# Hybrid decoder block on one core: the mixer's weight sums made beside the state space, one weight piece in its own place, norms in two steps

## The chip, the cores and the metric

One core of a Trainium2 chip runs the whole kernel. The metric is the device time of one execution in microseconds. The kernel before was timed in three runs; beside them stands one profiled execution, from which all lines of the profile are taken. The core has five instruction queues that run by themselves: TensorE (PE, matrix products into PSUM banks), VectorE (DVE), ScalarE (ACT), GpSimd (POOL) and SyncE (SP, which here only issues transfers). Transfers are issued on SP's and on ACT's queue and run on the core's 16 DMA engines. Each queue holds its instructions in a fixed order, and an instruction that waits holds back all behind it.

## The reference

One decoder layer on 1024 tokens of width 1024, in float32. The part around the change:

```python
u = rms_norm(h, norm_mix[l])
u_ssm, q, k, v, f_logit, gate_logits = jnp.split(u @ w_in[l], [...], axis=-1)
y_ssm = jax.nn.gelu(s5_ssm(u_ssm, ...))                  # diagonal state space, 32 groups
glu_a, glu_b = jnp.split(y_ssm @ w_glu[l], 2, axis=-1)
out_a = glu_a * jax.nn.sigmoid(glu_b)
out_b = forgetting_attention(q, k, v, f_logit + b_forget[l]) @ w_fox_o[l]
gate_a, gate_b = jnp.split(jax.nn.sigmoid(gate_logits), 2, axis=-1)
h = h + (gate_a * out_a + gate_b * out_b) @ w_mix_out[l]  # the mixer projection
h = h + memory_cross_attention(rms_norm(h, norm_mem_q[l]), ...)
f_a, f_b = jnp.split(rms_norm(h, norm_ffn[l]) @ w_ffn_in[l], 2, axis=-1)
h = h + (jax.nn.silu(f_a) * f_b) @ w_ffn_out[l]           # then a last rms_norm
```

## The kernel before

Tokens are kept in 8 tiles of 128 rows, or turned, features on the 128 partitions and tokens in two halves of 512. Every float32 product is made of three products of rounded parts: each operand is split into a high part (ACT rounds it, L178) and a low part (DVE subtracts, L179), and PE does high times high, low times high, high times low (L168 to L170; L602 in the mixer). A weight comes by `wload`: SP fetches it into a tile `raw` (two of them), ACT and DVE split it into `whi` and `wlo`. These two have a few slots each, so a split waits until PE has read the weight that had the slot.

Four stages follow each other. `stage_in` makes the norm and the first projections. `stage_ssm` makes the 32 gate blocks, 16 columns of 128 in two halves, each 24 matmuls of 512 columns, and hangs the state space (S5, four quarters q) between them: the table `todo` names the block ahead of which a step of S5 is written. In a quarter the transposes (`turn_weights`) give `Ts`, which three transfers on SP shift into a Toeplitz matrix, ACT copies it to `Tt` (L1427); `states` fetches `xg` and lets PE multiply it (L1440), DVE makes the recurrence; `out` multiplies `Tt` and `xg`. Fox (the forgetting attention) is next, and `stage_tail` does the rest.

`stage_tail` begins with a loop over j = 0 to 7 that makes the gated units (`glu`; `value` empties PE's bank with the DVE copy at L1166, `sigmoid` multiplies, L1172) and, three steps behind, the Fox projection `fox_part`, which adds the gated halves to `sg` and splits the result into the operands of the mixer. The mixer projection is a 2 x 2 block product with seven products instead of eight (`mix_mm(n, i)`: product n, block i of 4; `mix_add` adds it to the residual tiles H). Four of the products need sums of quarters of `w_mix_out`. They are made in the loop's first steps: `mix_fetch` reads two 512 KB pieces into the tiles with the tags `gbc` and `xs`, `mix_sums` adds quarters on DVE (L544) and ACT's queue stores them to `sums_d`, from where `mix_weights` loads them later like any weight. Both tiles have one slot, so the fetch of a step waits for the stores of the step before, and later uses of these tiles (`xm`, `s4`, the row `xs` of a norm) follow.

The last Fox parts, 5, 6 and 7, are woven into product 1. In parts j > 3 the second half's add runs on POOL (L564). The products then come in the order 1, 2, 6, 5, 3, 7, 4, and after each block one piece of `side` is written: the preparation of two columns of the forward network's weights (`ahead`: fetch `wpr`, sums on POOL, splits `wph` and `wpl` in slots of the pool `tmp`, stores to `w_d` on ACT's queue). The RMS norms ahead of the memory attention (`norm`) scale a row of H into `xs` on DVE (L217) and turn it on PE (L223). The norms of tiles 0 to 3 are written behind every second block of products 7 and 4, those of tiles 4 to 7 among the query projections.

## Time and profile before

| | us |
|---|---|
| median of 3 runs | 1615.45 (1613.74 to 1618.33) |
| the profiled execution | 1621.55 |
| its span, first to last instruction | 1619.8 |
| PE busy | 1534.7 (95%) |
| DVE busy | 1064.4 (66%) |
| ACT busy | 670.2 (41%) |
| POOL busy | 268.8 (17%) |
| mean granted clock of TensorE | 0.975 |

A row of the timeline has start, length, engine, line, operation, output <- inputs, shapes, and in brackets the idle time ahead of it on its engine and what ended it. A row of the waits has who waited and for whom, the total, how often, and the longest. A row of the windows has the stretch, its length, busy time and instructions of PE, PE's weight loads, DVE, ACT and POOL, then TensorE's granted clock, the busy share of the DMA engines and GB/s. The chain of waits has start, length and what it was. On SP a row spans the issues that it groups, with the waits between them.

### The profile page before, as it was taken

The page shows a single profiled execution, that of the slowest core. Times are in us where ns is not written, and L with a number is a line of the kernel's source. Part 1 is how long each engine was busy: PE and PEld are TensorE (multiplying, and loading weights), DVE is VectorE, ACT ScalarE, POOL GpSimd, SP SyncE. Part 2 cuts the span into 40 slices and gives each one's busy share as a digit, 9 for nine tenths or more (in the row PEclk, how much of TensorE's full clock was granted, in tenths as well). Part 3 has the DMA queues.
Part 4 walks back from the last instruction along what each step waited for, and adds up shares of the span by engine and source line. Part 5 has one row for each costly group of instructions (what it writes and reads, how often), then busy time and mean ns, then how long its engine had stood idle before and what let it go on. Part 6 is the DMA issues. An engine that isn't in the chain of part 4 may idle for free.

```text
span 1619.8 us, 20543 instructions
## 1 busy us (share of the span) xinstructions
PE 1534.7 (95%) x7301; PEld 1263.2 (78%) x7301; DVE 1064.4 (66%) x1882; ACT 670.2 (41%) x1191; POOL 268.8 (17%) x341
## 2 busy tenths in 40 slices
PE   5799999999999999697999999999999999999997
PEld 5688888898776678586787777888888888788886
DVE  5756555444777777687765687766766776466555
ACT  5422433323666642123445564333333333254342
POOL 3015443200211124123201210000100000000001
PEclk8899999999999999898999999999999999999999
DMA  8745446442124646857813168444454444796642
GB/s 268 141 93 92 126 131 113 120 137 29 34 43 72 170 127 205 289 186 282 275 53 104 53 223 303 149 150 156 157 166 159 150 162 149 241 393 231 195 156 104
DMA packets 202871, 258.71 MB, mean 160 GB/s; under 512 B 36024, under 2 KB 127064, under 8 KB 202256
## 3 DMA queue, kind: packets, MB, share of 16 engines
q1 hardware_dynamic: 193840, 237.47, 49.4%
q10 hardware_dynamic: 8928, 19.93, 3.2%
q8 instruction: 57, 0.93, 0.2%
q14 instruction: 46, 0.38, 0.1%
HBM read 176.08 MB, written 83.20 MB: 160 GB/s over the span
## 4 chain that ended last, share of the span: by engine, by line
PE 76%; DMA 7%; DVE 7%; issue 4%; ACT 3%; POOL 2%; SPq 1%; ACTq 0%; DVEq 0%; POOLq 0%
PE mm L947 15%; PE pv L947 7%; PE mm L168 7%; PE mm L169 7%; PE mm L170 7%; PE mm L1084 4%; PE sc L947 4%; PE sc L1084 3%; PE pv L1084 3%; PE sc L168 3%; PE sc L169 3%; PE sc L170 3%; PE misc L1084 1%; DMA mw<-in_w_mix_out_dram 1%; DMA or<-in_w_ffn_out_dram 1%
## 5 line engine op out<-in xcount | busy, mean ns | idle before, releaser
L179 DVE TENSOR_TENSOR wlo<-raw,whi 128x1024 fp32r<-128x1024 f32 (+2 forms) x127 | 138.3, 1093 | 115.4 <-ACT whi L178 114.8
L178 ACT CAST whi<-raw 128x1024 fp32r<-128x1024 f32 (+1 forms) x128 | 116.6, 914 | 169.9 <-PE mm L169 49.2
L168 PE MATMUL mm<-uh,whi 128*128 128x512 f32 x344 | 138.2, 402 | 2.4 <-ACT whi L178 2.3
L170 PE MATMUL mm<-uh,wlo 128*128 128x512 f32 x344 | 135.7, 395 | 0.0
L179 DVE TENSOR_TENSOR ol<-or,oh 128x1024 fp32r<-128x1024 f32 x73 | 89.4, 1224 | 70.5 <-ACT oh L178 69.4
L169 PE MATMUL mm<-ul,whi 128*128 128x512 f32 x344 | 135.7, 394 | 0.0
L178 ACT CAST oh<-or 128x1024 fp32r<-128x1024 f32 x73 | 76.7, 1051 | 104.4 <-PE mm L1084 35.0
L979 POOL TENSOR_TENSOR g<-a,c 128x512 f32<-128x512 f32 x22 | 35.6, 1617 | 397.2 <-ACT a L978 397.2
L1709 POOL TENSOR_TENSOR pl<-pf,ph 128x512 fp32r<-128x512 f32 (+1 forms) x32 | 39.5, 1234 | 243.1 <-DVE ph L1708 198.1
L168 PEld LDWEIGHTS mm<-uh,whi 128*128 128x128 f32 x344 | 65.5, 191 | 14.8 <-ACT whi L178 2.8
L170 PEld LDWEIGHTS mm<-uh,wlo 128*128 128x128 f32 x344 | 65.2, 190 | 14.6 <-DVE wlo L179 1.3
L169 PEld LDWEIGHTS mm<-ul,whi 128*128 128x128 f32 x344 | 65.5, 190 | 10.9
L197 POOL TENSOR_TENSOR r<-ms,mhalf 128x1 f32<-128x1 f32 (+1 forms) x30 | 17.8, 598 | 317.5 <-DVE ms L193 287.4
L1706 ACT ACTIVATE pf<-sc 128x512 f32<-128x512 f32 (+1 forms) x96 | 46.4, 490 | 49.6 <-DVE sc L1702 30.0
L947 PE MATMUL pv<-S3h,we 128*128 128x512 f32 x176 | 58.1, 389 | 0.0
L168 PE MATMUL mm<-yh,whi 128*128 128x512 f32 x104 | 41.7, 401 | 14.1 <-DVE sg L1166 14.1
L1179 POOL TENSOR_TENSOR sg<-sg,ga 128x512 f32<-128x512 f32 x16 | 30.3, 1919 | 87.0 <-DMA ga<-gate_d 43.8
L1712 DVE TENSOR_TENSOR pl<-pf,ph 128x512 fp32r<-128x512 f32 (+2 forms) x64 | 35.7, 558 | 10.1 <-ACT ph L1711 9.4
L170 PE MATMUL mm<-yh,wlo 128*128 128x512 f32 x104 | 41.3, 398 | 0.0
L169 PE MATMUL mm<-yl,whi 128*128 128x512 f32 x104 | 41.3, 397 | 0.0
L1084 PE MATMUL mm<-oh 128*128 128x512 f32 x106 | 41.3, 389 | 0.0
L1084 PE MATMUL mm<-ol,oh 128*128 128x512 f32 x106 | 41.3, 389 | 0.0
(667 smaller groups left out, 4615.4 us busy)
## 6 DMA issues: line engine op xcount, KB each, us to landing
or<-c_d SPq DMA_DIRECT2D x77, 256.0 KB
wo<-in_w_ffn_out_dram SPq DMA_DIRECT2D x22, 512.0 KB
c_d<-g SPq DMA_DIRECT2D x44, 256.0 KB
t_d<-wo SPq DMA_DIRECT2D x44, 256.0 KB
or<-t_d SPq DMA_DIRECT2D x44, 256.0 KB
raw<-in_w_ffn_in_dram SPq DMA_DIRECT2D x20, 512.0 KB
rawb<-in_w_ffn_in_dram SPq DMA_DIRECT2D x20, 512.0 KB
raw<-in_w_in_dram SPq DMA_DIRECT2D x18, 512.0 KB
```

What stands on the lines that cost most here:

```text
L168: T.matmul(ps, lh, rh, start=first, stop=False)
L169: T.matmul(ps, lh, rl, start=False, stop=False)
L170: T.matmul(ps, ll, rh, start=False, stop=last)
L178: self.A.copy(hi, src)
L179: (self.G if pool_lo else self.V).tensor_sub(lo, src, f32(hi))
L947: T.matmul(ps, l_[:, k, :], r_, start=first and k == 0 and i == 0, stop=k == 3 and i == 2, skip_group_check=True)
L979: G.tensor_mul(g[:, 512:], a1, c1)
L1084: T.matmul(ps, l_[:, gi], r_[:, 512:], start=n < 3 and p == 0 and k == 0 or n == 7 and p == 0 and k == 0, stop=p == NP - 1 and k == 2, ski ...
L1179: self.B.G.tensor_mul(self.out[j][:, cs], self.out[j][:, cs], ga)
L1706: self.exp = A.activation(pf[:, off:], ps[:, off:], AF.Exp)
L1709: G.tensor_sub(pl[:, off:], pf[:, off:], f32(ph[:, off:]))
L1712: V.tensor_sub(pl[:, off:], pf[:, off:], f32(ph[:, off:]))
```

## The change

The mixer's weight sums move from the first four steps of the loop in `stage_tail` to `stage_ssm`: ahead of gate block 7k stands the fetch of piece pair k, ahead of 7k + 2 its adds, ahead of 7k + 3 its stores, now on SP's queue. They have two tiles of their own there. To make room for them, tables that only the setup of S5 uses move to the pool that ends with `stage_in`. In the mixer, the first weight piece of product 1 gets tiles of its own (`w1h`, `w1l`), the loads of product 2's weight are written ahead of Fox part 7, the POOL add of the Fox parts becomes a DVE add, and the split of S1 is held back to the next part. A norm is cut in two: `scaled` (the DVE part, now into a slot of `tmp`) right behind the last sum of its tile, `turned` (the PE part) in product 7 and among the query projections. PE's count of matmuls is the same.

```diff
-    def wload(self, pieces, cols, pool_lo=False, behind=None):
+    def wload(self, pieces, cols, pool_lo=False, behind=None, into=None):
 
         raw = self.wpool.tile([P, RAW], F32, tag="raw", bufs=2, name="raw")
         for off, shape, src in pieces:
             n = shape[0] * shape[1]
             self.S.dma_start(raw[:, off:off + n].rearrange("p (k c) -> p k c", k=shape[0]), src)
-        hi = self.wpool.tile([P, WSLOT], F32R, tag="whi", name="whi")
-        lo = self.wpool.tile([P, WSLOT], F32R, tag="wlo", name="wlo")
+        hi, lo = into or [self.wpool.tile([P, WSLOT], F32R, tag=t_, name=t_) for t_ in ("whi", "wlo")]
...
+    mw = {}
+
+    def mix_fetch(k):
+        mw[k] = [qp.tile([P, D], F32, tag="mw", bufs=2, name="mw") for _ in range(2)]
+        for w_, r_ in zip(mw[k], (k, 4 + k)):
+            S.dma_start(w_, w_mix_out[r_ * P:(r_ + 1) * P, :])
+
+    def mix_parts(k):
+        (b11, b12), (b21, b22) = [(w_[:, :512], w_[:, 512:]) for w_ in mw[k]]
+        return (5, b11, b12), (7, b12, b22), (6, b22, b11), (4, b21, b22)
+
+    def mix_sums(k):
+
+        for _, o, i in mix_parts(k):
+            B.V.tensor_add(o, o, i)
+
+    def mix_store(k):
+        for n, o, _ in mix_parts(k):
+            S.dma_start(sums_d[n, k // 2][:, k % 2 * 512:k % 2 * 512 + 512], o)
+
...
+    for k in range(4):
+        for i, f in ((7 * k, mix_fetch), (7 * k + 2, mix_sums), (7 * k + 3, mix_store)):
+            todo.setdefault(i, []).append(lambda f=f, k=k: f(k))
     for i, f in enumerate(gates):
         for g in todo.get(i, []):
             g()
...
-    def mix_fetch(k):
-        mw[k] = [s2.tile([P, D], F32, tag=t_, bufs=1, name="mw") for t_ in ("gbc", "xs")]
-        for w_, r_ in zip(mw[k], (k, 4 + k)):
-            S.dma_start(w_, w_mix_out[r_ * P:(r_ + 1) * P, :])
-
-    def mix_sums(k):
-
-        w1, w2 = mw.pop(k)
-        b11, b12, b21, b22 = w1[:, :512], w1[:, 512:], w2[:, :512], w2[:, 512:]
-        for n, o, i in ((5, b11, b12), (7, b12, b22), (6, b22, b11), (4, b21, b22)):
-            V.tensor_add(o, o, i)
-            A.dma_start(sums_d[n, k // 2][:, k % 2 * 512:k % 2 * 512 + 512], o)
...
-            (G if j > 3 and h else V).tensor_add(sg[:, cs], sg[:, cs], gb)
+            if h and late:
+                late.pop(0)()
+            V.tensor_add(sg[:, cs], sg[:, cs], gb)
...
-        give("S1", bslot, k, x_[:, 512:])
         S.dma_start(s3_d[k // 2][:, k % 2 * 512:k % 2 * 512 + 512], s0)
+        late.append(lambda: give("S1", bslot, k, x_[:, 512:]))
...
-                hl = B.wload([(0, (2, 512), src)], D)
+                own = [s2.tile([P, D], F32R, tag=t_, bufs=1, name=t_) for t_ in ("w1h", "w1l")] if n == 1 and kk == 0 else None
+                hl = B.wload([(0, (2, 512), src)], D, into=own)
...
-    mix_fetch(0)
     for j in range(8):
         if j > 3:
             for f in glu.values(j):
                 f()
         glu.rest(j)
-        if j < 4:
-            mix_sums(j)
-            if j < 3:
-                mix_fetch(j + 1)
...
     fox_part(6)
     mix_mm(1, 2)
+    mix_weights(2)
     fox_part(7)
-    mix_weights(2)
...
-    def norm(t, gb, act, banks=("misc", "pv")):
-        xs = s2.tile([P, D], F32, tag="xs", bufs=1, name="xs")
-        B.norm_scale(xs, H[t], B.rstd(H[t]), gb)
-        B.norm_turn(xs, act, t, banks)
+    xss = {}
+
+    def scaled(t):
+        xss[t] = tmp("xs")
+        B.norm_scale(xss[t], H[t], B.rstd(H[t]), gq)
+
+    def turned(t, banks):
+        B.norm_turn(xss.pop(t), u2, t, banks)
...
     for n, m in ((2, 5), (6, 3), (5, 7), (3, 4), (7, None), (4, None)):
         for i in range(4):
             mix_mm(n, i)
-            if n in (7, 4):
-                if i % 2:
-                    norm(2 * (n == 4) + i // 2, gq, u2, ("mm", "misc"))
+            if n == 7:
+                turned(i, ("mm", "misc"))
+            mix_add(n, i)
+            if n in (3, 4):
+                scaled((n == 4) * 4 + i)
+            elif late:
+                late.pop()()
             elif side:
                 side.pop(0)()
-            mix_add(n, i)
...
-    weave([lambda h=h: mem_q(h, 0) for h in range(MH)], [lambda t=t: norm(t, gq, u2) for t in range(4, 8)])
+    weave([lambda h=h: mem_q(h, 0) for h in range(MH)], [lambda t=t: turned(t, ("misc", "pv")) for t in range(4, 8)])
...
-            self.rows = sp.tile([48, P], F32, name="prow")
+            self.rows = self.xp.tile([48, P], F32, name="prow")
...
```

Where instructions stand now is shown at three places, in the order of one engine's queue. The first is SP's queue in `stage_ssm`, in the first two quarters: `raw` are the gates' weights, `mw` the pieces of `w_mix_out`, `y_d` the quarter's output. Before:

```order
L153 DMA raw_1378<-in_w_in_dram 128x4x256
L1433 DMA xg_1412<-u_d_77 128x1024
L153 DMA raw_1646<-in_w_in_dram 128x4x256
L153 DMA raw_1652<-in_w_in_dram 128x4x256
L1422 DMA Ts_1366<-Ts_1366 112x128
L1422 DMA Ts_1366<-Ts_1366 96x256
L1422 DMA Ts_1366<-Ts_1366 64x512
L153 DMA raw_1976<-in_w_in_dram 128x4x256
L153 DMA raw_1982<-in_w_in_dram 128x4x256
L1433 DMA xg_1828<-u_d_77 128x1024
```

With the change, from the first shift of `Ts` on:

```order
L1439 DMA Ts_1379<-Ts_1379 112x128
L505 DMA sums_d_84<-mw_1629 128x512
L505 DMA sums_d_84<-mw_1630 128x512 x2
L1439 DMA Ts_1379<-Ts_1379 96x256
L492 DMA mw_2069<-in_w_mix_out_dram 128x1024
L492 DMA mw_2070<-in_w_mix_out_dram 128x1024
L1439 DMA Ts_1379<-Ts_1379 64x512
L505 DMA sums_d_84<-mw_2069 128x512 x2
L505 DMA sums_d_84<-mw_2070 128x512 x2
L492 DMA mw_2509<-in_w_mix_out_dram 128x1024
L492 DMA mw_2510<-in_w_mix_out_dram 128x1024
L153 DMA raw_2001<-in_w_in_dram 128x4x256
```

Stores and fetches now stand between the shifts, and ahead of the gates' weights; behind those, the four stores of the last pair (`mw_2509`, `mw_2510`) stand ahead of the second quarter's `xg`. The second place is DVE's queue at the last Fox part. Before, with `wlo_6942` the second piece of product 2, and `h0`, `h1` tiles of H:

```order
L563 TENSOR_TENSOR gb_6900<-gb_6900,pv_6887 128x512
L179 TENSOR_TENSOR wpl_7042<-wpr_7024,wph_7041 128x1024
L564 TENSOR_TENSOR sg_6611<-sg_6611,gb_6900 128x512
L609 TENSOR_TENSOR h0_6961<-h0_6961,mm_6733 128x512
L563 TENSOR_TENSOR gb_6919<-gb_6919,pv_6906 128x512
L609 TENSOR_TENSOR h1_6962<-h1_6962,mm_6734 128x512
L179 TENSOR_TENSOR A12l_6691<-sg_6611,A12h_6689 128x512
L575 SCALAR_TENSOR_TENSOR xm_6821<-sg_6611,xm_6821 128x512
L179 TENSOR_TENSOR wlo_6942<-raw_6939,whi_6941 128x1024
```

With the change (`wlo_6997` and `wlo_7003` belong to product 6):

```order
L573 TENSOR_TENSOR gb_6910<-gb_6910,pv_6897 128x512
L576 TENSOR_TENSOR sg_6611<-sg_6611,gb_6910 128x512
L622 TENSOR_TENSOR h0_6959<-h0_6959,mm_6727 128x512
L573 TENSOR_TENSOR gb_6929<-gb_6929,pv_6916 128x512
L178 TENSOR_TENSOR A12l_6691<-sg_6611,A12h_6689 128x512
L576 TENSOR_TENSOR sg_6611<-sg_6611,gb_6929 128x512
L178 TENSOR_TENSOR wlo_6997<-raw_6994,whi_6996 128x1024
L178 TENSOR_TENSOR A22l_6714<-sg_6611,A22h_6712 128x512
L587 SCALAR_TENSOR_TENSOR xm_6819<-sg_6611,xm_6819 128x512
L178 TENSOR_TENSOR wlo_7003<-raw_7000,whi_7002 128x1024
```

The second piece of product 2 is gone from here: it now stands in Fox part 5, some 20 rows earlier. The second add of `sg` is new on DVE, and one residual add still stands ahead of A12. The third place is DVE's queue at the first norms. Before, with `wlo_7345` and `wlo_7351` the pieces of product 4:

```order
L609 TENSOR_TENSOR h2_6963<-h2_6963,mm_6735 128x512
L609 TENSOR_TENSOR h3_6964<-h3_6964,misc_6736 128x512
L179 TENSOR_TENSOR wlo_7345<-raw_7342,whi_7344 128x1024
L193 TENSOR_SCALAR ms1_7383<-ss_7380 128x1
L203 SCALAR_TENSOR_TENSOR r01_7384<-rt1_7385,r01_7384 128x1
L179 TENSOR_TENSOR wlo_7351<-raw_7348,whi_7350 128x1024
L609 TENSOR_TENSOR h4_6965<-h4_6965,sc_6957 128x512
L217 SCALAR_TENSOR_TENSOR xs_7379<-h0_6961,r01_7384,gbc_6977 128x1024
```

With the change (`wlo_7389` and `wlo_7395` are the pieces of product 4):

```order
L622 TENSOR_TENSOR h2_6961<-h2_6961,mm_6729 128x512
L216 SCALAR_TENSOR_TENSOR xs_7295<-h0_6959,r01_7300,gbc_6975 128x1024
L216 SCALAR_TENSOR_TENSOR xs_7321<-h1_6960,r01_7326,gbc_6975 128x1024
L622 TENSOR_TENSOR h3_6962<-h3_6962,misc_6730 128x512
L178 TENSOR_TENSOR wlo_7389<-raw_7386,whi_7388 128x1024
L216 SCALAR_TENSOR_TENSOR xs_7347<-h2_6961,r01_7352,gbc_6975 128x1024
L178 TENSOR_TENSOR wlo_7395<-raw_7392,whi_7394 128x1024
L622 TENSOR_TENSOR h4_6963<-h4_6963,sc_6955 128x512
```

The scaled rows have moved ahead of product 4's weight splits, each into a tile of its own.

More of the change, by code (lines that the diff above doesn't have):

```diff
@@ L311, in hybrid_block_kernel @@
     kv_d = B.dram.tile([4, P, D], F32, name="kv_d")
+    sums_d = B.dram.tile([8, 2, P, D], F32, name="sums_d")
     big = ctx.enter_context(tc.tile_pool(name="big", bufs=16))
@@ L518, in load @@
         return t_
-    sums_d = B.dram.tile([8, 2, P, D], F32, name="sums_d")
     am_d = B.dram.tile([4, P, D], F32, name="am_d")
     s3_d = B.dram.tile([2, P, D], F32, name="s3_d")
-    fox, part, xm, mw, mixw, msets = {}, {}, {}, {}, {}, []
+    fox, part, xm, mixw, msets, late = {}, {}, {}, {}, [], []
     def operand(name, mk):
```

29 lines of the change are left out of this document (16 added, 13 removed).

## The prediction

> **What bounds the kernel now.** I read first the page's busy times, then TensorE's list of waits in the stretch where the change acts, then the timeline at each wait, then the chain behind it.
>
> ```profile
> span 1619.8 us, 20543 instructions
> PE 1534.7 (95%) x7301; PEld 1263.2 (78%) x7301; DVE 1064.4 (66%) x1882; ACT 670.2 (41%) x1191; POOL 268.8 (17%) x341
> PE mm L168 <- DVE sg L1166: 14.1, 1, 14.1
> PE sc L602 <- DVE wlo L179: 7.4, 1, 7.4
> PE mm L223 <- DVE xs L217: 3.1, 1, 3.1
> PE pv L1731 <- POOL pl L1709: 1.7, 1, 1.7
> ```
>
> TensorE (PE) is busy 95% of the span, and the change takes no matmul away. So the change can only win PE's idle time and the slow clock behind it. The last four lines are the longest PE waits between 575 and 960 us (total, times, longest): three stand out, 14.1, 7.4 and 3.1 us, and the fourth is already small and lies elsewhere. Each of the three is followed by matmuls that start further apart than usual:
>
> ```profile
> 675.39 0.80 PE L168 MATMUL mm<-yh,whi 128*128 128x512 f32 x1 [14.08 <-DVE sg L1166]
> 678.41 0.39 PE L169 MATMUL mm<-yl,whi 128*128 128x512 f32 x1
> 755.00 0.79 PE L602 MATMUL sc<-wlo,A12h 128*128 128x512 f32 x1 [7.44 <-DVE wlo L179]
> 760.23 0.39 PE L602 MATMUL sc<-wlo,A12h 128*128 128x512 f32 x1
> 760.46 0.40 PE L602 MATMUL sc<-whi,A12l 128*128 128x512 f32 x1
> 808.67 1.11 PE L223 MATMUL mm<-ident,xs 128*128 128x128 f32 x4 [3.13 <-DVE xs L217]
> 810.29 0.78 PE L602 MATMUL pv<-whi,S3l 128*128 128x512 f32 x1
> 814.97 0.39 PE L602 MATMUL pv<-wlo,S3h 128*128 128x512 f32 x1
> ```
>
> Two matmuls of this size normally start 0.23 us apart (760.23 to 760.46). From 675.39 to 678.41 there are 7 such steps, 3.0 us where 1.6 is normal: 1.4 us lost. From 755.00 to 760.23 there are 12: 5.2 against 2.8, 2.4 lost. From 810.29 to 814.97 there are 11: 4.7 against 2.5, 2.2 lost. So the three waits are worth 14.1 + 1.4 = **15.5**, 7.4 + 2.4 = **9.8** and 3.1 + 2.2 = **5.3 us**, together 30.6, and that is the most the change can win here. The Trainium skill ("TensorE: Matmul & The Clock Gate", What's actually happening) says that the clock drops to half after an idle window of about 3.4 us and returns after about 3.4 us of activity. By that rule each slow stretch would lose 1.7 us, 5.1 in all where the rows give 6.0, the most to win would be 29.7, and a wait of 3.13 us need not have slowed the clock; the rows show that it did, and decide here.
>
> **First wait, 15.5 us.** What holds the vector engine (DVE) before its copy at L1166:
>
> ```profile
> 664.42 3.09 DVE L544 TENSOR_TENSOR mw<-mw 128x512 f32<-128x512 f32 x3 [3.39 <-DMA mw<-in_w_mix_out_dram]
> 673.05 0.69 DVE L544 TENSOR_TENSOR mw<-mw 128x512 f32<-128x512 f32 x1 [0.93 <-issue]
> 674.26 1.07 DVE L1166 COPY sg<-mm 128x512 f32<-128x512 f32 x1
> ...
> 659.91 4.41 DMA mw<-in_w_mix_out_dram
> ...
> 665.15 4.20 DMA sums_d<-mw
> 669.41 2.11 DMA mw<-in_w_mix_out_dram
> ...
> 660.00:670.00 10.00, 1.31 (x6) 0.75 (x4) 6.51 (x8) 1.66 (x2) 3.29 (x2) 0.73 0.93 313
> ```
>
> The chain of waits (start, length, what) alternates: fetch a piece of the output weight, add on DVE, store the sum, only then fetch the next into the same tile. The adds stand in DVE's queue ahead of the copy that empties PE's bank, so PE stops while DVE waits for transfers: in 660 to 670 PE was busy 1.31 of 10 us, with a DMA share of 0.93. The change takes all of it from this place: 8 fetches, 16 adds, 16 stores. Between these adds DVE has only the work of the gated units and the Fox projection, which PE itself paces. I take **15.0** of 15.5 (between 11 and 15.5: a shorter wait for a gate tile or a split may appear, and the fourth row of the list, 1.7 us, is the nearest size of such a wait).
>
> **Second wait, 9.8 us.**
>
> ```profile
> 745.64 0.69 DVE L609 TENSOR_TENSOR h<-h,mm 128x512 f32<-128x512 f32 x1 [0.23 <-DMA h<-in_x_dram]
> 749.09 1.71 POOL L686 TENSOR_TENSOR wpr<-wpr 128x512 f32<-128x512 f32 x1
> 750.76 1.25 POOL L564 TENSOR_TENSOR sg<-sg,gb 128x512 f32<-128x512 f32 x1
> 752.05 0.69 DVE L575 SCALAR_TENSOR_TENSOR xm<-sg,xm 128x512 f32<-128x512 f32 x1 [2.37 <-POOL sg L564]
> 752.66 2.28 DVE L179 TENSOR_TENSOR wlo<-raw,whi 128x1024 fp32r<-128x1024 f32 x1
> ```
>
> The low half of mix 2's second weight piece (wlo) comes behind DVE's wait for the POOL add of the last Fox part, which itself queues behind the weight sums of the forward network on POOL. Two edits take both causes away: that add goes to DVE (0.69 us, like its neighbours), and the piece is split two parts earlier, because the first product's first piece no longer uses the shared pair. What is late next is the low half of A12 in the last Fox part: it still stands behind the residual add, which waits for its tile from x (745.64, 0.23 us here). PE's cover from the end of that part is the last block of mix 1 and the first half of mix 2's first block, 18 matmuls of 0.23, 4.1 us, and the tile's load is only issued when that part has freed its place. I take a rest of 1 us, so **8.8** (between 5.4, if the load lands later by one transfer such as the 4.41 us at 659.91, and 9.8).
>
> **Third wait, 5.3 us.**
>
> ```profile
> 805.59 1.22 DVE L179 TENSOR_TENSOR wlo<-raw,whi 128x1024 fp32r<-128x1024 f32 x1 [2.46 <-ACT whi L178]
> 807.34 1.28 DVE L217 SCALAR_TENSOR_TENSOR xs<-h,r,gbc 128x1024 f32<-128x1024 f32 x1
> 770.00:780.00 10.00, 10.00 (x46) 8.27 (x45) 6.62 (x11) 3.15 (x4) 0.00 (x0) 1.00 1.03 315
> ```
>
> The scaled row xs stands behind a weight split whose data came late. In the new order the first two scalings stand ahead of mix 4's splits and the third between them, and PE turns a row one full product (4 blocks, 10.9 us) after its sum is complete. But xs now takes a slot of the pool through which the forward network's prepared weights leave for memory, and here the DMA engines are full (1.03 from 770 to 780), all the more as PE arrives 10 us earlier. I take **3.5** of 5.3 (between a loss of 3, if the slot is as late again as this wait was long, and 5.3).
>
> **What the state-space stage pays.** The 8 MB (4 read, 4 written) and 16 adds now lie here:
>
> ```profile
> 100.00:280.00 180.00, 180.00 (x917) 153.31 (x916) 99.89 (x150) 65.26 (x102) 79.62 (x178) 1.00 0.54 120
> L544 DVE TENSOR_TENSOR mw<-mw x16: 669/693/1773, 632.5 to 678.6; 128x512 f32<-128x512 f32 x16
> 143.69 1.54 SPq L153 DMA_DIRECT2D raw<-in_w_in_dram  x2
> 145.75 14.51 SPq L1422 DMA_DIRECT2D Ts<-Ts  x3
> 162.19 1.05 ACT L178 CAST whi<-raw 128x1024 fp32r<-128x1024 f32 x1 [0.95 <-PE sc L169]
> 166.35 1.04 ACT L1427 COPY Tt<-Ts 128x1024 f32<-128x1024 f32 x1
> 179.98 1.51 SPq L153 DMA_DIRECT2D raw<-in_w_in_dram  x2
> 181.59 0.52 SPq L1433 DMA_DIRECT2D xg<-u_d  x1
> 193.01 1.95 PE L1440 MATMUL pv<-xg,F 128*128 128x128 f32 x16
> 176.00:178.00 2.00, 2.00 (x10) 1.68 (x9) 1.88 (x6) 1.14 (x1) 0.00 (x0) 1.00 0.00 0
> 188.00:192.00 4.00, 4.00 (x19) 3.31 (x18) 0.00 (x0) 1.05 (x1) 3.92 (x6) 1.00 0.97 368
> ```
>
> From 100 to 280 us PE never idles, DVE is busy 99.9 of 180 us and DMA 0.54. The adds cost 16 x 0.69 = 11 us of DVE, which its 80 idle us hold; 8 MB at 368 GB/s, the rate of the full stretch 188 to 192, take 22 us of the 83 that DMA has free. By volume the price is nothing. By order it is not: SP issues in sequence, and each store now there waits for adds, and each further fetch for stores. Two loads are near. First, the three shifts of Ts, issued over 14.5 us from 145.75 and needed by the copy at 166.35: three stores and 1 MB of fetches now lie between them. 1 MB at 368 GB/s is 2.8 us, against about 6 us from the last issue (160.3) to the copy: 0.5 us. Second, xg of the second quarter, issued at 181.59 for PE at 193.01, 11.4 us later: behind the gate weights there now stand four adds (2.8 us), four stores, 1 MB (2.8 us) and a fetch of 1 MB ahead of the weights (2.8 us), 8.4 us on top of a stretch in which DMA is full to 192. Some of the fetch falls into a time in which DMA rests (0.00 from 176 to 178). I take 2 us of PE wait. Together **2.5 us lost** (between 0 and 11: both delays in full, 8.4 and 2.8). The gate weights have cover: fetched at 143.69, split at 162.19 only when PE lets the tile go.
>
> The other edits I cost at nothing: four adds of 0.69 us move to DVE, which is idle a third of the span; the later split of S1 and the side work moved by one block have later readers by a whole product. Without that cover each is worth its 0.69 us.
>
> **Sum.** -15.0 - 8.8 - 3.5 + 2.5 = -24.8 us. The profiled execution took 1621.55 us, so it would be 1596.8. It lies 6.1 us above the median of the three runs, 1615.45; the difference, not the level, carries over: 1615.45 - 24.8 = **1590.7 us**, 1.5% faster.
>
> **Rivals.**
> - *Clean.* Stage idle time swallows all transfers and all three waits go: -30.6, 1584.8 us. For it: DMA 0.54 and DVE 55% in that stage. Against: the order on SP.
> - *The mixer becomes bound by transfers.* Without its pauses PE reaches 770 to 800 earlier, while DMA was full there already. The third wait stays whole and 4.4 of the second returns: -15.0 - 5.4 + 0 + 2.5 = -17.9, 1597.6 us. For it: 1.03 in 770 to 780. Against: those transfers are mostly weights for later, and a product's pieces are fetched a product ahead.
> - *Late operands in the state-space stage.* xg and Ts are wholly late: 11 us lost, -27.3 + 11 = -16.3, 1599 us. It decides from the point where xg lands after PE's gate blocks have run out, 11.4 us behind its issue.
> - *Slower: SP held before the gate weights.* A store waits for an add, the add for a fetch, the fetch for a store: 4.4 + 2 x 0.7 + 4.2 = 10 us for a round, by the rows of the chain above. If in each quarter a round stands ahead of the gate weights and their cover is gone, 4 x 10 = 40 us lost: -27.3 + 40 = +12.7, 1628 us. It decides from some 10 us of delay, since the weights issued at 143.69 wait until 162.19 and need about half of that to land. Against it: SP has nothing to issue for most of a quarter, and only the first three quarters hold such rounds.
> - *Nothing gained.* The copy at L1166 would be late for another reason, a gate tile or a weight split, and PE waits as long: 1613 to 1615 us. Against it: the chain above, without a gap, through the adds.
>
> **How the numbers follow.** Forecast 0.52 (1586 to 1596); mixer bound by transfers 0.18; clean 0.12; late operands 0.08; slower 0.06; nothing gained 0.04. The range from 1582 to 1604 holds the first four with their own spread, 0.9 less their tails. About 0.3% of the time, 4.8 us, is what a measurement can tell from no change; faster by more than that 0.88, within it 0.06, slower 0.06.
>
> **What would show it.** In the changed profile: no PE wait for sg at L1181 over 2 us; the wait of sc for wlo gone, at most a short one for A12l or a whole tile of x; the wait for xs under 2 us; PE's share between 100 and 280 us below 100% by 2 to 3 us, with the matmuls that read xg of the second quarter behind it. I am wrong in size if PE idles more than 5 us there, or if the mixer's products wait for weight splits; wrong in kind if DVE's copy still comes late without the adds.

## The result, and the profile after

The changed kernel takes **1602.79 us** (median of 6 runs, 1599.0 to 1608.22), the kernel before on the same chip 1616.59 (6 runs): ratio 0.9918, 95% interval 0.9894 to 0.9941, so 13.8 us or 0.8% faster. The profiled execution took 1599.39 us. Its page begins:

```profile
span 1597.6 us, 20547 instructions
PE 1533.2 (96%) x7301; PEld 1260.2 (79%) x7301; DVE 1069.6 (67%) x1886; ACT 671.1 (42%) x1191; POOL 266.1 (17%) x337
```

TensorE's list of waits between 560 and 940 us (who waited, for whom; total, times, longest):

```profile
PE mm L615 <- ACT S4h L177: 3.5, 1, 3.5
PE pv L1748 <- POOL pl L1726: 1.7, 1, 1.7
PE misc L222 <- DVE u2l L178: 1.2, 1, 1.2
```

The three waits of before (14.1, 7.4 and 3.1 us) are gone. The line at the top is new: in product 3 PE waits for the operand S4. The window of the loop that stood still before, and the whole state-space window:

```profile
660.00:670.00 10.00, 10.00 (x45) 8.26 (x44) 9.43 (x11) 3.94 (x5) 0.79 (x1) 1.00 0.34 116
100.00:280.00 180.00, 175.01 (x872) 147.85 (x871) 108.87 (x161) 59.53 (x95) 78.55 (x177) 0.99 0.61 156
```

In 660 to 670 PE is busy 10.00 of 10 us (1.31 before) and the DMA share fell from 0.93 to 0.34. In 100 to 280 PE was busy all 180 us before; now it idles 5.0, and does 45 matmuls fewer in that time. Its waits there, between 90 and 330 us:

```profile
PE pv L1426 <- ACT m L1504: 2.3, 1, 2.3
PE pv L1500 <- ACT Tt L1444: 2.0, 1, 2.0
PE pv L1457 <- DMA xg<-u_d: 0.7, 1, 0.7
```

Two of the three come from ACT, one from a transfer. ACT's and SP's timelines at that place (start, length; in brackets the idle time ahead and what ended it):

```profile
172.15 0.60 ACT L476 ACTIVATE gs<-mm 128x512 f32<-128x512 f32 x1 [1.62 <-DMA sums_d<-mw]
185.25 0.33 ACTq L477 DMA_DIRECT2D gate_d<-gs  x1
185.66 1.28 ACT L1504 ACT_TABLE_LOAD   x1 [12.91 <-DMA mw<-in_w_mix_out_dram]
...
169.64 11.62 SPq L505 DMA_DIRECT2D sums_d<-mw  x4
181.35 2.23 SPq L492 DMA_DIRECT2D mw<-in_w_mix_out_dram  x2
186.40 5.02 SPq L505 DMA_DIRECT2D sums_d<-mw  x4
```

ACT finished a gate block at 172.75 and could not issue its store until 185.25: it stood 12.9 us, until a fetch of `mw` that SP had issued landed, though the store reads nothing of it. In the kernel before, ACT's row at the same place had no such wait:

```profile
171.62 1.28 ACT L1487 ACT_TABLE_LOAD   x1 [0.44 <-ACT gs L475]
```

The compiled program says why. Two of its instructions on the two queues, with the semaphores that they wait for:

```
ACT  L477 DMA gate_d<-gs 128x512 [waits DMAHW2_49,Activation_49]
SP   L505 DMA sums_d<-mw 128x512 [waits DMAHW1_49,DVE_49]
```

The transfers of both queues share eight completion semaphores (DMAHW0 to DMAHW7), and a transfer that takes one over waits until the one before it on that semaphore has landed. The two instructions show the kind of wait; the gate store at 185.25 itself takes over DMAHW3, which the fetch of the last pair's first piece (`mw_2509`) had used before it. So SP's slow rounds of fetch, add and store hold ACT's queue, and behind the gate store stand the gelu and the copies that PE needs.

DVE's queue carries the delay as well. The adds stand in it between the steps of S5, and an add whose fetch has not landed holds all that follows:

```profile
150.42 1.42 DVE L501 TENSOR_TENSOR mw<-mw 128x512 f32<-128x512 f32 x2 [2.73 <-DMA mw<-in_w_mix_out_dram]
```

Between 90 and 330 us DVE stood 13.9 us for fetches of `mw` (three times, the longest 9.0), where the kernel before has no such wait. The chain of waits behind the first quarter's recurrence runs through this add and the fetch ahead of it (145.66, 4.67 us), and the recurrence ends later: ACT's copy `r`, which waits for it, starts 42.6 us after the first gate block's activation, 37.6 before, and the copy to `Tt`, for which PE waits 2.0 us, is 5.0 us later too. The other way round, SP's four stores at 169.64 stood 11.62 us, since DVE reached three of their adds only from 178.42 on, behind a wait of 6.81 us for POOL.

The other new wait, by the chain of waits (start, length, what), PE's timeline and the windows ahead of it:

```profile
758.40 6.33 DMA raw<-in_w_mix_out_dram
764.73 9.93 DMA s<-s_d
774.69 0.63 ACT S4h L177
```

```profile
775.36 0.50 PE L615 MATMUL mm<-whi,S4h 128*128 128x512 f32 x1 [3.50 <-ACT S4h L177]
777.77 0.80 PE L615 MATMUL mm<-whi,S4l 128*128 128x512 f32 x1 [0.72 <-DVE S4l L178]
783.66 0.48 PE L615 MATMUL mm<-whi,S4h 128*128 128x512 f32 x1
```

```profile
750.00:760.00 10.00, 10.00 (x46) 8.29 (x45) 9.52 (x13) 4.78 (x8) 1.29 (x1) 1.00 0.99 350
760.00:770.00 10.00, 10.00 (x46) 8.29 (x45) 6.93 (x10) 3.46 (x5) 0.00 (x0) 1.00 0.96 308
```

The second half of S4 has landed 9.93 us after SP turned to its load (SP's own row of that load takes 4.00 of them), while the DMA engines are full (0.99 and 0.96). PE idles 3.50 and 0.72 us, and then runs slowly: 13 matmul steps from 777.77 to 783.66 take 5.9 us where 13 x 0.23 = 3.0 is normal.

In the kernel before, the same half was split just in time. Its split on ACT and PE's first product with it:

```profile
786.09 1.15 ACT L178 CAST S4h<-s 128x512 fp32r<-128x512 f32 x2 [1.33 <-DMA s<-s_d]
789.97 0.39 PE L602 MATMUL mm<-whi,S4h 128*128 128x512 f32 x1
```

The first of its two blocks was ready at about 786.7, 3.3 us before PE came. Counted from the first matmul of product 2 (744.85 before, 736.42 now), PE came to it after 45.1 us and would now come after 35.3, 9.8 us sooner, which is the length of the second wait; the split began after 41.2 us and now begins after 38.3. So S4 is not later than before; PE's wait in product 2 had covered it. The full engines have their part as well: the load took 6.2 us before (779.85 to 786.09), and 3.7 us less now would by estimate have spared PE the wait for S4h.

**Stage by stage.** The table is worked out from the timeline of each profiled execution: a stage lasts from the start of its first matmul to the first of the next (us). Product 6, between 2 and 5, took 10.88 us in every kernel and is left out. "Gates" is the state-space stage, "loop" the glu loop with product 1, "mem q" the query projections and the first half of the memory attention. The last rows are the experiments below. Rows come from different chips, on which the kernel before took 1612.96 to 1616.59 us, so the ratios compare them better than the medians do.

```
kernel      median   ratio [95% interval]      gates   Fox    loop   prod2 prod5 prod3 prod7 prod4 mem q
before      1616.59                            206.49 218.06 129.94 22.00 10.88 10.88 18.81 13.84 62.45
after       1602.79  0.9918 [0.9894, 0.9941]   213.80 218.45 114.24 12.15 10.88 18.90 16.17 11.98 58.90
sums_only   1608.90  0.9967 [0.9955, 0.9979]   212.65 217.22 114.30 21.98 10.88 10.88 17.02 13.85 62.26
no_sums     1607.75  0.9957 [0.9939, 0.9974]   206.40 215.81 130.36 12.17 10.94 18.76 15.11 11.94 58.99
mw_four     1599.03  0.9903 [0.9881, 0.9925]   213.49 217.85 114.24 12.45 11.23 19.10 16.40 11.97 58.94
held        1609.91  0.9970 [0.9955, 0.9986]   220.74 218.22 114.24 11.94 10.88 17.99 16.98 11.97 59.25
held_later  1610.66  0.9970 [0.9955, 0.9985]   220.72 218.28 114.23 12.01 10.88 12.47 19.20 11.52 64.94
gate_sp     1605.30  0.9944 [0.9926, 0.9963]   216.60 218.35 114.30 11.75 10.88 17.66 16.73 11.98 58.97
fox_sums    1597.61  0.9893 [0.9873, 0.9913]   206.40 218.86 114.24 11.98 10.88 16.62 19.77 11.95 59.04
fox_pool    1600.57  0.9911 [0.9891, 0.9931]   206.40 224.31 114.24 11.86 10.88 19.40 15.57 11.98 58.92
s4_two      1604.22  0.9934 [0.9911, 0.9956]   213.78 218.73 114.24 12.49 10.88 11.01 24.33 11.93 59.01
later       1604.52  0.9937 [0.9917, 0.9957]   214.87 218.73 114.24 12.72 10.88 11.86 19.20 11.52 64.35
old_norm    1610.56  0.9972 [0.9954, 0.9990]   213.87 216.95 114.24 12.06 10.88 17.89 16.15 14.85 63.83
s1_back     1598.84  0.9899 [0.9881, 0.9918]   206.41 220.80 114.24 10.88 12.90 19.31 18.38 11.93 59.02
```

From before to after: loop -15.7, product 2 -9.9, product 3 +8.0, product 7 -2.6, product 4 -1.9, mem q -3.6, gates +7.3, together **-18.3 us**. Stages that no edit touches differ too: the middle of the forward network took 421.2 to 425.4 us over these kernels, with the same instructions, and the Fox stage 215.81 to 218.73 in those without the sums in it. So one profiled pair settles a stage to a few tenths where PE never stops, the gates to about 1 us (213.78 to 214.87 in the four kernels that share them), but the whole time only to some 5 us.

### The profile page after: what moved, and what is told of

It reads as the page before. It is cut to its first block, busy times and chain, and to the rows that moved or that the text cites. A ratio compares the mean times of both kernels' runs of the same rounds, so it can differ in the third digit from the quotient of the medians.

```text
span 1597.6 us, 20547 instructions
## 1 busy us (share of the span) xinstructions
PE 1533.2 (96%) x7301; PEld 1260.2 (79%) x7301; DVE 1069.6 (67%) x1886; ACT 671.1 (42%) x1191; POOL 266.1 (17%) x337
## 4 chain that ended last, share of the span: by engine, by line
PE 78%; DVE 8%; DMA 5%; POOL 3%; issue 3%; ACT 2%; SPq 1%; DVEq 0%; ACTq 0%; POOLq 0%
PE mm L962 15%; PE pv L962 7%; PE mm L167 7%; PE mm L168 7%; PE mm L169 7%; PE mm L1099 4%; PE sc L962 4%; PE sc L1099 3%; PE pv L1099 3%; PE sc L167 2%; PE sc L169 2%; PE sc L168 2%; PE misc L1099 1%; PE pv L167 1%; PE pv L169 1%
## 5 line engine op out<-in xcount | busy, mean ns | idle before, releaser
L178 DVE TENSOR_TENSOR wlo<-raw,whi 128x1024 fp32r<-128x1024 f32 (+2 forms) x126 | 134.8, 1072 | 113.9 <-ACT whi L177 113.5
L177 ACT CAST whi<-raw 128x1024 fp32r<-128x1024 f32 (+2 forms) x127 | 115.6, 914 | 140.7 <-PE mm L168 43.6
L1099 PE MATMUL mm<-ol,oh 128*128 128x512 f32 x106 | 41.2, 389 | 0.0
L1099 PE MATMUL mm<-oh,ol 128*128 128x512 f32 x106 | 41.2, 389 | 0.0
L1099 PE MATMUL mm<-oh 128*128 128x512 f32 x106 | 41.2, 389 | 0.0
L167 PE MATMUL sc<-uh,whi 128*128 128x512 f32 x104 | 40.8, 393 | 0.0
```

The costliest lines, as they stand in the source:

```text
L167: T.matmul(ps, lh, rh, start=first, stop=False)
L177: self.A.copy(hi, src)
L178: (self.G if pool_lo else self.V).tensor_sub(lo, src, f32(hi))
L1099: T.matmul(ps, l_[:, gi], r_[:, 512:], start=n < 3 and p == 0 and k == 0 or n == 7 and p == 0 and k == 0, stop=p == NP - 1 and k == 2, ski ...
```

## Experiments

Ratios are against runs of the kernel before on the same chip.

**The parts alone.** `sums_only` is the kernel before with the moved sums and nothing else; `no_sums` is the change with the sums back in the loop.

```diff
+    for k in range(4):
+        for i, f in ((7 * k, mix_fetch), (7 * k + 2, mix_sums), (7 * k + 3, mix_store)):
+            todo.setdefault(i, []).append(lambda f=f, k=k: f(k))
...
-        if j < 4:
-            mix_sums(j)
-            if j < 3:
-                mix_fetch(j + 1)
```

> The kernel before with one part of the change: the weight sums (and the S5 tables that make room) moved to the state-space stage; Fox parts, weight pieces and norms as before. Theory A, the parts add up: the first wait goes (15.7 us from the first sigmoid product of the gated units to the last, as in the changed kernel), the stage between 100 and 320 us grows by 7.3, so about 8.4 us faster than before, 0.995; the waits for wlo (7.4) and xs (3.1) stay. Theory B, the first wait was only a buffer and its time comes back at the next wait: wlo's wait grows and the kernel is no more than 3 us faster.

> The change without the moved sums: they are made in the tail as before; everything else as changed. Theory A, the new wait for S4 (3.5 us and a slow clock, 8 us in the profile) comes from S4's single tile and its place one block later: it is there again, the wait of 14.1 us is there again, wlo's is gone, and the kernel is about 10 us faster than before (0.994). Theory B, S4 is late because TensorE arrives some 15 us earlier in a stretch where the DMA engines are full: here TensorE arrives later, S4's wait is under 1 us, and the kernel is about 18 us faster (0.989).

TensorE's waits between 560 and 960 us, first `sums_only`, then `no_sums`:

```profile
PE sc L613 <- DVE wlo L178: 7.3, 1, 7.3
PE mm L222 <- DVE xs L216: 2.6, 1, 2.6
```

```profile
PE mm L167 <- DVE sg L1198: 13.3, 1, 13.3
PE mm L627 <- ACT S4h L177: 2.2, 1, 2.2
PE mm L627 <- DVE S4l L178: 1.8, 2, 1.1
```

Each part removes its own waits and leaves the other's in place. The moved sums win 15.6 us in the loop and lose 6.2 in the gates; the rest wins 9.8 in product 2 and 3.5 in mem q and loses 7.9 in product 3; products 7 and 4 give 3.7 and 1.9. The two ratios together, 0.33% and 0.43%, make 0.76%, close to the change's 0.82%. S4 is late in `no_sums` too, so its lateness does not come from the earlier arrival that the sums bring.

**More tiles for the sums.** `mw_four` gives `mw` four tiles, so that a fetch no longer waits for the stores of the pair before.

```diff
-        mw[k] = [qp.tile([P, D], F32, tag="mw", bufs=2, name="mw") for _ in range(2)]
+        mw[k] = [qp.tile([P, D], F32, tag="mw", bufs=4, name="mw") for _ in range(2)]
```

> The changed kernel with four tiles for the pieces of the output weight in the state-space stage in place of two, so that a fetch no longer waits for the stores of the pair before. Theory A, the 7.3 us that the stage grew hang on that wait (ScalarE stood 12.9 us at a gate store behind the last pair's fetch, and the GELU, the transposes and xg came late behind it): the 12.9 us go and the stage grows by under 3 us, 4 to 7 us faster than the changed kernel. Theory B, the 8 MB themselves crowd the stage: the same 7 us, at other waits, and the time stays within 1.5 us of the changed kernel.

ACT's wait ahead of the gelu is gone, but the gates take 213.49 us. ACT's timeline and, below it, PE's only wait there:

```profile
144.75 0.60 ACT L476 ACTIVATE gs<-mm 128x512 f32<-128x512 f32 x1 [5.83 <-PE mm L169]
156.66 0.33 ACTq L477 DMA_DIRECT2D gate_d<-gs  x1
157.02 0.74 ACT L1462 COPY zre<-pv 64x256 f32<-64x256 f32 x2 [11.68 <-DMA raw<-in_w_in_dram]
```

```profile
PE pv L1500 <- ACT Tt L1444: 4.5, 1, 4.5
```

ACT now stands at a gate store 29 us earlier, for nearly as long (11.68 us, until a gate weight landed), and the state's copies behind it are late; PE then waits for the Toeplitz copy. The tile that fetches waited for was not the price: with it gone, the queue is held at another store. The ratio, 0.9903 against 0.9918 with overlapping intervals, shows no gain over after, and no stage of the profiled pair does.

**The sums' transfers held behind the state space's own.** In `held` a fetch is issued behind the quarter's output stores, the adds behind Ts's add, the stores behind the third shift.

```diff
-        for i, f in ((7 * k, mix_fetch), (7 * k + 2, mix_sums), (7 * k + 3, mix_store)):
-            todo.setdefault(i, []).append(lambda f=f, k=k: f(k))
+        for i, f, m_ in ((7 * k + 2, mix_fetch, "last_s" if k else None), (7 * k + 5, mix_sums, "ts_v"), (7 * k + 5, mix_store, "ts_s")):
+            todo.setdefault(i, []).append(lambda f=f, k=k, m_=m_: put(f, k, m_))
```

> The changed kernel with the sums' transfers held in place in each quarter of the state-space stage: the fetch behind the y stores of the quarter before, the adds behind DVE's add into Ts, the stores behind the third shift of Ts; nothing stands between the shifts or ahead of xg. The same bytes and adds. Theory A, the stage's 7 us come from the order on SP's queue (stores and fetches between the shifts of Ts, ahead of xg, and gate stores that wait for them): the gate blocks' stage (213.8 us in the profile of the changed kernel, 206.5 before) returns to 206.5 to 208, and the kernel is 5 to 7 us faster than the changed one, 0.987 to 0.989 of before. Theory B, the 8 MB and the adds themselves crowd the stage: it stays above 211 us.

The theory that only SP's order was wrong fell: gates 220.74 us, 7 worse. ACT's timeline in `held` shows a gate block computed at 178.68 whose store is issued at 191.91, and the copies of F behind it:

```profile
178.68 0.60 ACT L476 ACTIVATE gs<-mm 128x512 f32<-128x512 f32 x1 [2.47 <-PE mm L169]
191.91 0.33 ACTq L477 DMA_DIRECT2D gate_d<-gs  x1
192.84 0.58 ACT L1431 COPY F<-pv 128x512 f32<-128x512 f32 x1
```

**Gate stores off ACT.** `gate_sp` issues them on SP.

```diff
-        A.dma_start(gate_d[j * P:(j + 1) * P, 512 * h:512 * h + 512], gs)
+        S.dma_start(gate_d[j * P:(j + 1) * P, 512 * h:512 * h + 512], gs)
```

> The kernel after with the sums in the state-space stage, and the gate blocks' stores issued on SP's queue instead of ACT's. Theory A (ACT stood 12.9 us at a gate store behind the sums' transfers, and what followed on ACT came late): ACT's long wait shrinks to under 5 us, the gate stage takes 208 to 210 us, time 1598 to 1600 us. Rival B (the sums' volume and their place between the shifts of Ts are the price, ACT's wait only beside it): gate stage 213 to 214 us, time as after. Rival C (SP now waits for each gate's activation, and holds the shifts, xg and weights): gate stage 216 us or more, slower than after.

Rival C held: gates 216.60 us. ACT's and PE's waits between 90 and 330 us:

```profile
ACT gs L476 <- DMA gate_d<-gs: 37.1, 6, 11.4
...
PE pv L1457 <- ACT whi L177: 5.9, 1, 5.9
```

The store now stands in SP's queue behind the sums, and the activation waits for its tile `gs` instead. The wait changes its place and stays. What these three leave as it was is DVE's stand: it waits 9.7 us for fetches of `mw` in `mw_four`, 18.2 in `held` and 12.4 in `gate_sp`. No run here parts DVE's share of the stage's 7.3 us from ACT's.

**The sums in the Fox stage.** `fox_sums` makes them beside Fox's heads 0 to 3, in tiles of Fox's pool; `fox_pool` the same with the adds on POOL.

```diff
+            if h in (0, 1, 2, 3):
+                k = (0, 1, 2, 3).index(h)
+                side[0].append(lambda k=k: mix_fetch(k))
+                for n in range(4):
+                    side[6 + n].append(lambda k=k, n=n: mix_sum(k, n))
+                side[10].append(lambda k=k: mix_store(k))
...
-            B.V.tensor_add(o, o, i)
+            B.G.tensor_add(o, o, i)
```

> The kernel after, but the weight sums stand in the Fox stage instead of the state-space stage: for heads 0 to 3 the fetch with the head's first score block, one add each with blocks 6 to 9, the four stores with block 10, on SP. Theory A (the 7 us that the state-space stage lost are the price of the sums' transfers between its own; in the Fox stage the DMA share is 0.1 to 0.4 and neither SP nor ACT issues much): the gate stage returns to 206.4 us from 213.8, Fox grows by at most 2 us, time 1594 to 1598 us. Rival B (the price goes along with the sums: each add stands in DVE's queue of the Fox stage, where DVE is busy 75% and PE waits for the scores): Fox grows by 5 us or more, 1600 to 1604 us. Rival C (the state-space stage loses its 7 us to something else in the change): gate stage stays above 211 us.

> As the run before, with the sixteen adds on POOL, which is busy 18% in the Fox stage, instead of DVE. If the adds cost nothing there (theory A), the same time within 2 us, Fox within 1 us. If DVE's queue is what pays (rival B), Fox is shorter by 2 to 5 us than with the adds on DVE. If POOL pays instead (its add takes 1.25 us where DVE takes 0.69, and POOL makes the low halves for which PE waits), Fox is longer by 2 us or more.

The state-space window of `fox_sums`, and PE's longest wait in the Fox stage of `fox_pool`:

```profile
100.00:280.00 180.00, 180.00 (x917) 153.33 (x916) 98.94 (x147) 64.18 (x100) 76.78 (x177) 1.00 0.53 118
```

```profile
PE pv L1725 <- POOL pl L1703: 5.6, 2, 3.9
```

Theory A held: PE is busy all 180 us again, and gates are back at 206.40. DVE waits only 0.8 us for fetches of `mw` in the Fox stage. That stage takes 218.86 us, 0.4 more than in after, and 220.80 in `s1_back` below, which has the same sums; its own spread of some 3 us allows no closer price. The 7.3 us were the price of the sums in the state-space stage. At **1597.61 us** (0.9893, 0.9873 to 0.9913) this is the fastest median of the study, 1.1% under before; against after (0.9894 to 0.9941) the intervals overlap, and what speaks for it is the stage. On POOL the adds delay the low halves of the scores (5.6 us against 1.7), and Fox takes 5.4 us more than in `fox_sums`, 3.5 more than in `s1_back`.

**S4's tile, and the column's work.** Both halves of S4 pass through one tile, `xs`. `s4_two` gives the second half another. `later` instead writes the second column's preparation behind the mixer, among the query projections, and S4 one place earlier.

```diff
-        y = s2.tile([P, D], F32, tag="xs", bufs=1, name="s4")
+        y = s2.tile([P, D], F32, tag=("xs", "w1h")[kk], bufs=1, name="s4")
```

```diff
-            elif side:
+            elif len(side) > 5:
                 side.pop(0)()
...
-[lambda t=t: turned(t, ("misc", "pv")) for t in range(4, 8)])
+[lambda t=t: turned(t, ("misc", "pv")) for t in range(4, 8)] + side)
```

> The changed kernel with a second tile for the second half of S4 (the place of the first product's weight piece, free by then), so that its load need not wait until the first half is split. Theory A, the single tile makes it late: the wait for S4h (3.5 us, with the slow clock 8) goes, about 8 us faster than the changed kernel. Theory B, the full DMA engines make it late: the load is issued some 10 us earlier, but other transfers slide behind it (a weight split or wpr), and less than 3 us are won.

> The changed kernel with the second column of the forward network's weights prepared behind the mixer, among the query projections, in place of between the products; S4's loads follow the first column. Theory A, the time that TensorE loses in products 3 and 7 (8.0 us for S4; with a second tile for S4 8 us moved to xs) is set by that side work, which stands ahead of S4's splits, the residual adds and xs on DVE and ACT and waits for its transfers and POOL: both waits go, products 3 and 7 take 10.9 and about 14.5 us (18.9 and 16.2 in the changed kernel), 8 to 10 us less, unless the memory attention pays it back. Theory B, full DMA engines alone make S4 late: its transfers are as many, product 3 keeps more than 4 us of wait.

In `s4_two` product 3 takes 11.01 us, and product 7 takes 24.33. PE's waits there, and the chain of waits behind them:

```profile
PE misc L222 <- DVE h L622: 3.8, 1, 3.8
PE mm L222 <- DVE xs L216: 3.2, 1, 3.2
```

```profile
754.38 6.45 DMA w_d<-wpl
761.71 7.94 DMA wpr<-in_w_ffn_in_dram
769.67 1.06 ACT wph L177
```

The 8 us only moved to the next product: the second column's store and fetch (6.45 and 7.94 us) carry the same chain to the scaled rows. With that work later, product 3 is down to 11.86 us and mem q pays 5.4 back, but product 7 grows to 19.20 (the two together 31.1 us against 35.1). Its wait in `later`:

```profile
PE misc L222 <- DVE h L622: 3.3, 1, 3.3
```

From 773 us on no transfer stands in the chain of this wait, which ends at 790.65. PE turns a row into a bank (`misc`) that the last residual add of product 3 has to empty, and on DVE that add now stands behind the steps of the scaled rows and a weight split. The same wait is 1.0 us in after, 3.8 in `s4_two` and 2.8 in `fox_sums`; before and `old_norm` have none, so it looks like a price of the split norm itself, though no run takes it apart. Neither kernel is faster than after.

**Both together.** `held_later` joins `held` and `later`.

> Both edits, the sums' transfers held in place and the second column's side work behind the mixer. If the two losses are apart from each other, both gains add: 13 to 17 us faster than the changed kernel, 0.981 to 0.984 of before. If the second only moves to the memory attention or the forward network, no better than the held kernel alone.

It shows each one's stages and gains nothing over `held`.

**The split norms undone.** `old_norm` scales and turns a row in one step again, in its old places.

```diff
-            if n in (3, 4):
-                scaled((n == 4) * 4 + i)
+            if n in (7, 4):
+                if i % 2:
+                    norm(2 * (n == 4) + i // 2, gq, u2, ("mm", "misc"))
```

> The changed kernel with the norms in one step as before (rows scaled into the single tile and turned behind every second block of products 7 and 4). Theory A, the norm's split is worth what products 7, 4 and the query projections lost by it in the profile: product 7 18.8 in place of 16.2, product 4 13.8 in place of 12.0, query projections to memory output 62.4 in place of 58.9, 8 us in all, so this kernel is about 8 us slower than the changed one, close to 0.997 of before. Theory B, with S4's wait of 8 us ahead of it xs has time enough, and the split is worth under 4 us.

Product 4 grows by 2.9 and mem q by 4.9 us, 7.8 in all, and the median is 7.8 above that of after. Product 7, where the third wait stood, takes 16.15 us, as in after (16.17). Product 3 waits for S4 again (2.7 us), so the split norms are not what makes S4 late.

**The split of S1 back in its place**, on top of `fox_sums`; the side work and S4 then stand one block earlier.

```diff
-            if h and late:
-                late.pop(0)()
...
+        give("S1", bslot, k, x_[:, 512:])
-        late.append(lambda: give("S1", bslot, k, x_[:, 512:]))
```

> The kernel with the sums in the Fox stage, and one more edit taken back: the split of S1 stands in its own Fox part again, so that the side work and the loads of S4 behind it stand one block (2.7 us of PE) earlier in the mixer. Theory A (product 3 waits for S4 because the change moved that work by one block, which the prediction priced at nothing): products 3 and 7 together take 33 to 34 us instead of 36.4, the wait for S4h is 1 us or gone, time 1594 to 1596 us. Theory B (the wait is set by the full transfers between 750 and 775 us, ahead of which PE now arrives 14 us earlier; one block more or less does not matter): products 3 and 7 together 35.5 us or more, time within 1.5 us of 1597.6. If the split of S1 in its old place is late for A12 or for a weight piece again, product 2 grows from 12.0 us by 1 us or more, and the time goes up with it.

Theory B held: products 3 and 7 take 37.7 us (36.4 in `fox_sums`), and product 5 loses 2 more, product 2 wins 1.1. Its windows show the full transfers ahead of PE's wait for S4h (2.9 us, at 771):

```profile
750.00:760.00 10.00, 8.27 (x37) 6.54 (x36) 7.18 (x11) 4.28 (x6) 0.00 (x0) 1.00 0.95 363
760.00:770.00 10.00, 8.47 (x38) 6.68 (x36) 4.06 (x5) 2.55 (x3) 1.07 (x1) 1.00 1.01 361
```

## Why the prediction was right in kind and too large

The forecast was 24.8 us, to 1590.7; measured are 13.8, to 1602.79. All three waits went, and two losses took nearly half of the gain. That the time still lies in the stated range, near its slower end, is in part luck: losses in the mixer and in the state-space stage came together, which no rival had put in one sum, and 4.6 us that the third wait gave beyond its term paid for some of them.

- **First wait, -15.0 forecast.** The loop became 15.7 us shorter; PE does not stop in it. Right, and shown by `sums_only` and `no_sums` from both sides.
- **Second wait, -8.8.** Product 2 became 9.9 us shorter. What was to be late next, the low half of A12, costs 0.4 us. Right in what the wait itself is worth; that POOL's add and the piece's place both had to go was not taken apart.
- **Third wait, -3.5.** Products 7 and 4 and mem q lost 2.6, 1.9 and 3.6 us, 8.1 together, and `old_norm` gives 7.8. Mis-sized, and not where the forecast had it: the wait for xs stood in product 7, but undoing the split leaves product 7 as it is and costs product 4 and mem q. The forecast counted one wait. The rows of before had two more in mem q, behind the norms and in the attention:

```profile
PE mm L168 <- ACT u2h L178: 0.9, 1, 0.9
PE misc L772 <- DVE ptl L179: 1.6, 1, 1.6
```

Neither is in that stage after the change, and `old_norm` has both back (0.9 and 1.6 us). What makes product 7 shorter, if not the split, was not tried; with PE held at S4 just ahead of it, xs has more time.

- **What the sum lacked: product 3, +8.0.** This is the step that failed. The sum took the three waits as independent and let nothing else come last in the mixer. The rival "the mixer becomes bound by transfers" had the mechanism, full DMA engines as PE comes earlier, but priced it at the third wait and in product 2. It came at S4, whose halves pass through one tile behind full transfers. What the rival held against itself, that a product's pieces are fetched a product ahead, is true of the weights and not of S4: its second half was split 3.3 us before PE came, and PE now comes 9.8 us sooner. So the second wait was worth its 9.9 us only until S4. `no_sums`, where product 2 is as short, has the wait; `sums_only`, where product 2 still holds PE 10 us, has S4 split 3.5 us ahead of PE and no wait. `s4_two`, `later` and `s1_back` show that neither the tile nor the place of the side work alone is to blame: freed at one point, PE waits at the next, for the second column's chain or for the last residual add of product 3. Which of the edits that shorten product 2 (its loads ahead of Fox part 7, the own tiles, the add on DVE) is needed for that was not tried apart.
- **State-space stage, +2.5.** It lost 7.3 us, within the bounds of 0 to 11: a term mis-sized. Counted were xg (2 us; it is 0.7) and Ts (0.5; it is 2.0). Not counted was ACT: gate stores were not seen as tied to SP's transfers, and behind a stand of 12.9 us on ACT stood work for which PE waited 2.3 us. The adds were priced as 11 us of DVE's 80 idle ones; that DVE also stands for their fetches (13.9 us), with the recurrence behind it, was not counted, and the 2.0 us at Ts come that way. PE idles 5.0 us there, where 2 to 3 were to be seen. `fox_sums` shows the whole price, `mw_four`, `held` and `gate_sp` that neither more tiles nor two other orders took it away within that stage: a gate store or its tile stands for 11 to 13 us in each. Of the rival that ends slower, SP held before the gate weights, nothing is seen: no PE wait there names them.
- **"The difference, not the level, carries over."** The profiled pair differs by 1621.55 - 1599.39 = 22.2 us, its touched stages by 18.3, the medians by 13.8. The profiled execution of before lay 5.0 us above the median of the six runs (6.1 above that of the first three) and that of after 3.4 below. Of the 3.9 us between 22.2 and 18.3, 3.6 lie in the middle of the forward network (424.8 and 421.2 us), which no edit touches. The terms taken from the profiled execution held in the stages; why the medians show some 4.5 us less than the stages stays open. `sums_only` shows the same: -11.5 in its touched stages (gates, loop, products, mem q), -4.1 between the medians on its chip and -5.3 by the ratio (its expectation had 8.4).
- **The clock.** The prediction weighed the rule of the Trainium skill ("TensorE: Matmul & The Clock Gate", What's actually happening), an idle window of about 3.4 us. Here steps after waits of 3.50 and 0.72 us were slow until 783.66. And after a wait of only 2.3 us the granted clock of the state-space stage fell as well:

```profile
180.00:190.00 10.00, 7.66 (x45) 6.44 (x44) 7.65 (x15) 4.31 (x6) 0.00 (x0) 1.00 0.93 265
190.00:200.00 10.00, 9.35 (x44) 7.75 (x44) 6.82 (x9) 4.44 (x7) 5.49 (x6) 0.83 1.02 350
```

This row alone does not settle it: behind the wait stand 3 us of transposes and 32-column products (187.70 to 190.67), and no run here shows whether the clock counts them as activity. In `gate_sp` PE waits 2.83 us between full products:

```profile
779.37 0.80 PE L615 MATMUL mm<-whi,S4h 128*128 128x512 f32 x1 [2.83 <-ACT S4h L177]
```

The step behind it takes 0.60 us instead of 0.23, at a granted clock of 0.50. The measurement decides: a wait shorter than the rule's window was enough. In the state-space stage of after, 5.0 us of waits became 7.3.

## What to carry to other kernels

A stall that is removed is worth its length only until the next operand on a full transfer path is late: ask for each product which of its operands lands last, not only which wait stands in the list now. Work with transfers goes to a stage in which both the DMA engines and the queues that issue are idle; a busy share of 0.54, which leaves room by volume, says little, since a transfer on one queue can hold another queue through shared semaphores, and an add that waits for its fetch holds its engine. And a rival's mechanism should be priced at every place where it can act.

## What the runs showed that was not expected

- A queue can stand for a transfer that it has no data from: ACT 12.9 us at a gate store, until SP's fetch of `mw` landed.
- Moving 16 adds of 0.69 us from DVE, busy 73% in the Fox stage, to POOL, busy 18%, made that stage 5.4 us longer (3.5 against the other kernel with the adds on DVE): the engine with more room was the one with the shorter cover.
- A 512 KB load (S4's second half) landed 9.93 us after its queue turned to it, with the DMA share at 0.96 between 760 and 770 us. In the kernel before, the same load took 6.2 us (779.85 to 786.09).
